# Reordering the scan of a Mamba-2 layer against its own state sums, its norm and its output projection

## The chip, the core and the metric

The kernel runs on one core of one Trainium2 chip. The metric is the device time of one execution in microseconds (us); three runs of the kernel before gave 1718.06, 1718.95 and 1721.03, median 1718.95. Times of single instructions come from one profiled execution.

## What is computed

One step of a two-layer backbone over 384 tokens (128 context tokens, then 256 latent tokens), width 1024. Layer 0 is FFN, latent attention, FFN; layer 1 is FFN, a bidirectional Mamba-2 scan (SSD), FFN. The change lies wholly in the scan. Cut to what matters:

```python
z, xbc, dt_raw = split(h @ w_in)              # h: normed input, 384 tokens
xbc = silu(conv5(xbc) + bias)                 # depthwise, then split into xs, B, C
dt  = softplus(dt_raw + dt_bias);  cum = cumsum(dt * a)      # per direction, per chunk of 128
y_diag = ((C B^T) * exp(seg(cum))) @ (xs * dt)               # inside a chunk, both directions
states = B^T @ (decay_end * dt * xs)                         # what a chunk adds to the state
h_next = h_in * exp(cum[-1]) + states                        # from chunk to chunk
y = y_diag + (C * exp(cum)) @ h_in + dsum * xs               # 2048 channels
out = rmsnorm(y * silu(z), norm_g) @ w_out                   # norm over the 2048 channels
```

The context is one chunk per direction, starting from zero; the latent tokens are two chunks, starting from a state that is given. The states of the context are an output.

## The kernel before, in words

Activations lie transposed: 128 channels on the partitions, 384 tokens along the free axis. Every weight passes through TensorE exactly once, from one stream of 512 KB units: SyncE loads a unit into `raw` (4 buffers), ScalarE rounds it into `whi` (L109), VectorE subtracts for the rest `wlo` (L110), 3 buffers each. `wmm` (L119 to L128) takes the 128 x 128 pieces of the stream in the order in which the program calls it and makes three products from each (L124, L125, L126); the host packs the weights in that order. An `in_tile` (L275) is 24 such products, one 128-channel tile of the input projection.

The 2048 channels of the scan are 16 tiles, `tau` = 0 to 15, of two heads each; four tiles share a group with one B and one C. The loop at L827 has steps `s` and is a software pipeline written out by hand:

- step `s` projects and convolves the x tile `s` (`conv`, L648, with L657 on VectorE; from step 2 on the projection of tile `s+1` is made ahead) and, every fourth step, the next group's B and C (`group_tiles`);
- `silu_z` evacuates and activates a z tile (L643, L791; table loads with it);
- `xtok(s-1)` transposes x to token order (L776), copies it (L778) and makes `xw`, weighted by decay, on GpSimd (L782);
- `mwork(s-1)` makes the decay matrix of a tile: three `seg` products (L765, L766), Exp on ScalarE (L767), two multiplications on VectorE (L768, L769), and C times decay into `cp` (L771);
- `ssd(s-2)` does all that is left of a tile: the state sums `pst` on TensorE (L801), their copy out, the next chunk's state `h1` on VectorE (L807, L809), and then at once the y products: those inside a chunk (L813), those with the given state `h` and those with `h1` (both L819). VectorE adds the skip term (L822), GpSimd multiplies with silu(z) into `yz` (L823);
- `loads(s)` asks SyncE for the next tile's decay rows (`segl`, `segr`), `cp` and `h0`.

In step 1 `dt_post` turns `dtt` (softplus, times a) into sums and decays: transposes (L714), small sums (L719, L720, L737 to L739), eight writes to `seg_d` (L730). After it come `loads(0, 1)`.

After the loop (L860 to L896): 16 pairs `yh`, `yl` of operands for the output projection (L864 on ScalarE, L865 on VectorE), then 16 squares (ScalarE, L869 and L872) that GpSimd adds into `yacc` (L873), then the projection `so`: the first 14 of 16 pieces of four output tiles, `rstd` after the third of them (its six small products are L216), `spread`, then the last two pieces of each and four whole tiles.

The program order is only a priority: a scheduler at compile time writes each engine's queue, taking what it reckons ready first. On the chip each engine then works its queue strictly in order.

Of the kernel before, what the change touches and what calls it, by code (L numbers as in the profile page):

```python
# [15 lines left out]
P = 128  # L16
# [37 lines left out]
def kernel(ctx, tc, xT_d, wstream, mod01, modw, crow_d, cst_d, tab_d, rope_d, ckvT_d, krT_d, h0_d,  # L54
# [11 lines left out]
    def bank(name):  # L66
        return psum.tile([P, 512], F32, tag="ps", name=name)
# [528 lines left out]
    def ssm(nxt):  # L596
# [11 lines left out]
        def mt(shape, tag, bufs=1, dt=F32):  # L608
            return sp.tile(shape, dt, tag=tag, name=tag, bufs=bufs)

        def keyf(m, k):
            return ("si", m, k)

        MZ, MX, MB, MC, MDT = 0, 16, 32, 36, 40
        dtt = mt([P, NTOK], "dtt")
        eb = mt([P, 3, 4, P], "E", 2)
        e1, e2, e3 = eb[:, 0].rearrange("p a b -> p (a b)")[:, 0:NTOK], eb[:, 1].rearrange("p a b -> p (a b)")[:, 0:NTOK], \
            eb[:, 2].rearrange("p a b -> p (a b)")[:, 0:NTOK]
        segr = [mt([P, 4, NTOK], f"segr{i}", 1, F32R) for i in range(2)]
        segl = [mt([P, NTOK], f"segl{i}", 1, F32R) for i in range(2)]  # L620
        ident16, mask16 = mt([P, P], "ident16", 1, BF16), mt([P, 4, P], "mask16", 1, BF16)

        def seg_init():
# [53 lines left out]
        tt(out=e2, in0=e2, in1=e1, op=ALU.mult)  # L677
        stt(out=dtt, in0=dtt, scalar=0.0, op0=ALU.max, in1=e2, op1=ALU.add)
        tt(out=dtt, in0=dtt, in1=e3, op=ALU.add)
        seg = mt([P, NTOK], "seg")  # L680
        ts(out=seg[64:128, :], in0=dtt[64:128, :], scalar1=1e-37, scalar2=None, op0=ALU.max)
        act(seg[64:128, :], seg[64:128, :], AF.Ln)
        seg_init()
# [21 lines left out]
            nc.scalar.copy(cb.rearrange("p a b -> p (a b)"), pc[:, 0:NTOK])  # L705
            grp[g] = [bT, cT, btok, cb]

        dtok = mt([P, 3, P], "dtok")
        dcy = mt([P, 2, 3, 32], "dcy")

        def dt_post():
            pt = bank("dtT")
            for c in range(3):
                nc.tensor.transpose(pt[:, c * P:(c + 1) * P], dtt[:, c * P:(c + 1) * P], T("ident"))  # L714
            nc.vector.tensor_copy(dtok.rearrange("p a b -> p (a b)"), pt[:, 0:NTOK])
            pr = bank("cumr")
            for c in range(3):
                da = dtok[:, c, 64:128]
                mm(pr[0:32, c * P:(c + 1) * P], da[:, 0:32], T("triu"), start=True, stop=True)  # L719
                mm(pr[32:64, c * P:(c + 1) * P], da[:, 32:64], T("tril"), start=True, stop=True)  # L720
            ecumr = mt([64, NLAT], "ecumr")
            segh, segt = mt([P, NTOK], "y", 2, F32R), mt([P, NTOK], "y", 2, F32R)
            nc.vector.tensor_copy(seg[0:64, :], pr[0:64, 0:NTOK])
            nc.scalar.copy(segh, seg)
            tt(out=segt, in0=seg, in1=segh, op=ALU.subtract)
            for half in range(2):
                for hl, s in ((0, segh), (1, segt)):
                    for d in range(2):
                        p0 = half * 64 + d * 32
                        nc.sync.dma_start(seg_d[:, half, hl, d], s[p0:p0 + 32, :].bitcast(F32))  # L730
            act(ecumr, pr[0:64, NCTX:NTOK], AF.Exp)
            nc.scalar.dma_start(ecum_d, ecumr)
            pc = bank("cum")
            for d, rest in enumerate(("slo", "sup")):
                cols = slice(64 + 32 * d, 96 + 32 * d)
                o = 96 * d
                mm(pc[:, o:o + 32], T(rest), dtok[:, 0, cols], start=True, stop=True)  # L737
                mm(pc[:, o + 32:o + 64], T(rest), dtok[:, 1 + d, cols], start=True, stop=True)
                mm(pc[:, o + 64:o + 96], T("ones"), dtok[:, 1 + d, cols], start=True, stop=True)  # L739
            act(dcy.rearrange("p a b c -> p (a b c)"), pc[:, 0:192], AF.Exp)  # L740
            for d in range(2):
                for ci, c in enumerate((0, 1 + d)):
                    tt(out=dcy[:, d, ci, :], in0=dcy[:, d, ci, :], in1=dtok[:, c, 32 * d:32 * d + 32], op=ALU.mult)
# [3 lines left out]
        def loads(*taus):  # L747
            for tau in taus:
                nc.sync.dma_start(segl[tau % 2][2:18, :].bitcast(F32), seg_d[tau].rearrange("a b c d t -> (a b c d) t"))
                nc.sync.dma_start(segr[tau % 2][0:2].bitcast(F32), seg_d[tau, 0].rearrange("b c d t -> b (c d) t"))  # L750
            for tau in taus:
                cp[tau] = mt([P, 2, 2, NLAT], "cp", 2)
                for d in range(2):
                    src = ecum_d[d * 32 + 2 * tau:d * 32 + 2 * tau + 2, :]
                    nc.sync.dma_start(cp[tau][:, d], src.partition_broadcast(P))
                h0[tau] = mt([P, 2, P], "h0", 2)
                nc.sync.dma_start(h0[tau], h0_d[:, :, tau * P:(tau + 1) * P])

        def mwork(tau):
# [27 lines left out]
        def silu_z(pz):  # L787
            tz = evac(pz)
            zs = mt([P, NTOK], "zs", 3)
            for s, a, b in SEGS:  # L790
                act(zs[:, a:b], tz[:, a:b], AF.Silu, bias=tz[:, NTOK + s:NTOK + s + 1])  # L791
            return zs

        def ssd(tau, zs):
            g = tau // 4
            btok = grp[g][2]
            w, xt, h = xw[tau], xtk[tau], h0[tau]
            pst = bank("st")
            for d in range(2):
                for ci, c in enumerate((0, 1 + d)):  # L800
# [2 lines left out]
            sto = mt([P, 2, P], "sto", 2)  # L803
            nc.scalar.copy(sto.rearrange("p a b -> p (a b)"), pst[:, 0:256])
            nc.sync.dma_start(state_d[:, :, tau * P:(tau + 1) * P], sto)
            h1 = mt([P, 2, P], "h1", 2)
            tt(out=h1.rearrange("p d (h q) -> p d h q", h=2), in0=h.rearrange("p d (h q) -> p d h q", h=2),  # L807
               in1=dcy[:, :, 2, 2 * tau:2 * tau + 2].unsqueeze(3).to_broadcast([P, 2, 2, 64]), op=ALU.mult)
            tt(out=h1.rearrange("p a b -> p (a b)"), in0=h1.rearrange("p a b -> p (a b)"), in1=pst[:, 256:512], op=ALU.add)  # L809
            py = bank("y")  # L810
            for c in range(3):
                for hh in range(2):
# [8 lines left out]
            y = mt([P, NTOK], "y", 2)  # L821
            stt(out=y, in0=xc[tau], scalar=dsum[:, tau:tau + 1], op0=ALU.mult, in1=py[:, 0:NTOK], op1=ALU.add)  # L822
            nc.gpsimd.tensor_tensor(out=yz[:, tau, :], in0=y, in1=zs, op=ALU.mult)  # L823

        group_tiles(0, pb, pc0)
        px = {0: px0}
        for s in range(NTAU + 2):  # L827
            if s < NTAU:
                if s % 4 == 0 and s > 0:
                    group_tiles(s // 4)  # L830
                xc[s] = mt([P, NTOK], "xc", 4)
                conv(px.pop(s) if s in px else in_tile(keyf, MX + s), s, xc[s])
                if s == 1:
                    z_first = [silu_z(in_tile(keyf, MZ))]
                    with tc.high_priority(60):
                        dt_post()
                    loads(0, 1)
                    z_first.append(silu_z(in_tile(keyf, MZ + 1)))
            if 2 <= s < NTAU - 1:
                px[s + 1] = in_tile(keyf, MX + s + 1)  # L840
            if s >= 2:
                zs = z_first[s - 2] if s < 5 else silu_z(in_tile(keyf, MZ + s - 2))
            if 1 <= s <= NTAU:
                if (s - 1) % 4 == 0:
                    group_post((s - 1) // 4)
                xtok(s - 1)
            if s == 2:
                z_first.append(silu_z(in_tile(keyf, MZ + 2)))
                mwork(0)
            if 2 <= s <= NTAU:  # L850
                mwork(s - 1)
            if s >= 2:
                ssd(s - 2, zs)
            if 2 <= s < NTAU:
                loads(s)
        inner.close()
        next_prep(nxt)
        gate = sec(layer, 5)
        yp = outer.enter_context(tc.tile_pool(name="ssmy", bufs=1, reuse_waits="tile"))
        yh, yl = [], []  # L860
        for k in range(NTAU):
            yh.append(yp.tile([P, NTOK], F32R, tag=f"yh{k}", name=f"yh{k}"))
            yl.append(yp.tile([P, NTOK], F32R, tag=f"yl{k}", name=f"yl{k}"))
            act(yh[k], yz[:, k, :], AF.Copy, scale=C("ssm_g", k))  # L864
            stt(out=yl[k], in0=yz[:, k, :], scalar=C("ssm_g", k), op0=ALU.mult, in1=yh[k], op1=ALU.subtract)  # L865

        for k in range(NTAU):
            if k == 0:
                act(yacc, yz[:, k, :], AF.Square)  # L869
            else:  # L870
                sq = yp.tile([P, NTOK], F32, tag="sqy", name="sqy", bufs=2)
                act(sq, yz[:, k, :], AF.Square)  # L872
                nc.gpsimd.tensor_tensor(out=yacc, in0=yacc, in1=sq, op=ALU.add)  # L873

        def so(ps, m, ks):
            for k in ks:
                wmm(ps[:, :NTOK], ("so", m, k), yh[k], yl[k], k == 0, k == NTAU - 1)

        def fin(m, ps):
            t = yp.tile([P, NTOK], F32, tag="t", name="tso", bufs=2)  # L880
            tt(out=t, in0=ps[:, :NTOK], in1=rext[:, :NTOK], op=ALU.mult)
            residual(m, t, gate, nxt)

        pso = [bank(f"so{m}") for m in range(4)]
        for m in range(4):
            so(pso[m], m, range(14))
            if m == 2:
                spread = rstd(yacc, 1.0 / 2048.0, rext[:, 0:NTOK])
        spread()
        for m in range(4):  # L890
# [211 lines left out]
```

## Time and profile before

| what | value |
|---|---|
| median of three runs | 1718.95 us |
| the profiled execution's own time | 1718.74 us |
| its span, first to last instruction | 1717.0 us |
| TensorE busy | 1662.9 us (97%) |
| VectorE busy | 1253.8 us (73%) |
| ScalarE busy | 798.2 us (46%) |
| GpSimd busy | 198.5 us (12%) |
| mean granted TensorE clock | 0.986 of full speed |

The 1.7 us between the profiled execution's time and its span lie outside the instructions. Busy time counts an engine as busy while an instruction of it runs; TensorE's own speed depends on the granted clock besides, which is shown for stretches of the span. The scan layer lies between about 1060 and 1400 us of the span.

### The profile page before, as it was taken

The page shows a single profiled execution, that of the slowest core. Times are in us where ns is not written, and L with a number is a line of the kernel's source. Part 1 is how long each engine was busy: PE and PEld are TensorE (multiplying, and loading weights), DVE is VectorE, ACT ScalarE, POOL GpSimd, SP SyncE. Part 2 cuts the span into 40 slices and gives each one's busy share as a digit, 9 for nine tenths or more (in the row PEclk, how much of TensorE's full clock was granted, in tenths as well). Part 3 has the DMA queues.
Part 4 walks back from the last instruction along what each step waited for, and adds up shares of the span by engine and source line. Part 5 has one row for each costly group of instructions (what it writes and reads, how often), then busy time and mean ns, then how long its engine had stood idle before and what let it go on. Part 6 is the DMA issues. An engine that isn't in the chain of part 4 may idle for free.

```text
span 1717.0 us, 25236 instructions
## 1 busy us (share of the span) xinstructions
PE 1662.9 (97%) x9616; PEld 1589.8 (93%) x9631; DVE 1253.8 (73%) x2069; ACT 798.2 (46%) x1312; POOL 198.5 (12%) x180
## 2 busy tenths in 40 slices
PE   7999999999999999999999999989999799999996
PEld 4899999978899999999999999878898799999996
DVE  3798889569768887976888896777877665444443
ACT  3534333455554333334333334877667744333332
POOL 0111100100001111000111000012212601111000
PEclk9999999999999999999999999899999999999998
DMA  8576666433246665765666674434444233333431
GB/s 345 172 230 211 209 206 219 132 137 111 76 170 188 203 207 190 231 211 173 204 208 203 200 229 150 123 105 132 128 139 120 84 124 122 123 125 124 132 124 49
DMA packets 88441, 281.99 MB, mean 164 GB/s; under 512 B 9836, under 2 KB 19900, under 8 KB 87808
## 3 DMA queue, kind: packets, MB, share of 16 engines
q1 hardware_dynamic: 86560, 274.26, 49.6%
q0 software_dynamic: 1104, 5.28, 0.9%
q8 instruction: 75, 1.23, 0.3%
q10 hardware_dynamic: 656, 0.85, 0.1%
q14 instruction: 46, 0.38, 0.1%
HBM read 276.06 MB, written 4.28 MB: 163 GB/s over the span
## 4 chain that ended last, share of the span: by engine, by line
PE 86%; DVE 5%; ACT 4%; DMA 2%; issue 2%; POOL 1%; SPq 0%; DVEq 0%; ACTq 0%; POOLq 0%
PE in L124 17%; PE in L126 17%; PE in L125 17%; PE fo L126 7%; PE fo L125 7%; PE fo L124 7%; DVE ca L657 2%; DMA cp<-ecum_d 1%; POOL yacc L873 1%; PE so L124 1%; PE so L125 1%; PE so L126 1%; ACT L767 1%; DVE wlo L110 1%; PE psmod L141 1%
## 5 line engine op out<-in xcount | busy, mean ns | idle before, releaser
L124 PE MATMUL in<-xh,wlo 128*128 128x386 f32 x1792 | 613.0, 343 | 3.1 <-ACT xh L246 3.1
L109 ACT CAST whi<-raw 128x1024 fp32r<-128x1024 f32 x348 | 365.2, 1050 | 539.2 <-issue 210.2
L126 PE MATMUL in<-xh,whi 128*128 128x386 f32 x1792 | 610.8, 341 | 0.0
L125 PE MATMUL in<-xl,whi 128*128 128x386 f32 x1792 | 607.9, 339 | 0.2 <-DVE xl L248 0.2
L110 DVE TENSOR_TENSOR wlo<-raw,whi 128x1024 fp32r<-128x1024 f32 x348 | 436.8, 1255 | 137.8 <-ACT whi L109 137.5
L124 PEld LDWEIGHTS in<-xh,wlo 128*128 128x128 f32 x1792 | 339.3, 189 | 10.9 <-issue 5.9
L125 PEld LDWEIGHTS in<-xl,whi 128*128 128x128 f32 x1792 | 340.0, 190 | 4.3 <-issue 1.8
L126 PEld LDWEIGHTS in<-xh,whi 128*128 128x128 f32 x1792 | 337.9, 189 | 4.9 <-issue 4.9
L125 PE MATMUL fo<-al,whi 128*128 128x384 f32 x704 | 236.7, 336 | 0.0
L124 PE MATMUL fo<-ah,wlo 128*128 128x384 f32 x704 | 236.7, 336 | 0.0
L126 PE MATMUL fo<-ah,whi 128*128 128x384 f32 x704 | 236.7, 336 | 0.0
L183 DVE CUSTOM_DVE_ANT_0 work<-modraw,crow,cst 128x1024 f32<-128x1024 f32 x144 | 185.2, 1287 | 21.7 <-POOL al L327 20.5
L327 POOL TENSOR_TENSOR al<-work,ah 128x384 fp32r<-128x384 f32 x88 | 109.5, 1244 | 739.4 <-ACT ah L326 726.0
L125 PEld LDWEIGHTS fo<-al,whi 128*128 128x128 f32 x704 | 132.0, 187 | 0.0
L126 PEld LDWEIGHTS fo<-ah,whi 128*128 128x128 f32 x704 | 132.0, 187 | 0.0
L124 PEld LDWEIGHTS fo<-ah,wlo 128*128 128x128 f32 x704 | 132.0, 187 | 0.0
L183 DVE CUSTOM_DVE_ANT_0 workout<-modraw,crow,cst 128x1024 f32<-128x1024 f32 x96 | 123.0, 1281 | 7.2 <-DMA modraw<-in_modw_dram 5.7
L326 ACT CAST ah<-work 128x384 fp32r<-128x384 f32 x88 | 45.3, 514 | 139.7 <-DVE work L324 139.7
L319 DVE TENSOR_TENSOR work<-in,rext 128x386 f32<-128x386 f32 x88 | 49.1, 558 | 67.6 <-PE in L126 65.8
L320 DVE TENSOR_TENSOR work<-in,rext 128x386 f32<-128x386 f32 x88 | 48.8, 554 | 45.3 <-PE in L126 45.3
L322 ACT ACTIVATE work<-work 128x128 f32<-128x128 f32 (+1 forms) x176 | 70.6, 447 | 6.0 <-DVE work L319 5.6
L324 DVE SCALAR_TENSOR_TENSOR work<-work 128x128 f32<-128x128 f32 (+1 forms) x176 | 68.0, 426 | 5.6 <-DVE work L320 0.5
(249 smaller groups left out, 1695.7 us busy)
## 6 DMA issues: line engine op xcount, KB each, us to landing
raw<-in_w_dram SPq DMA_DIRECT2D x348, 512.0 KB, 3.9
modraw<-in_modw_dram SPq DMA_DIRECT2D x128, 512.0 KB, 4.5
mod<-in_mod_dram SPq DMA_DIRECT2D x16, 512.0 KB, 9.5
cp<-ecum_d SPq DMA_DIRECT2D x32, 256.0 KB, 4.2
crow<-silu_d POOLq DMA_DIRECT2D x4, 1024.0 KB, 6.1
h<-in_h_dram SPq DMA_DIRECT2D x16, 128.0 KB, 4.3
out_dram<-sto SPq DMA_DIRECT2D x16, 128.0 KB, 2.2
xT<-in_xT_dram SPq DMA_DIRECT2D x4, 384.0 KB
```

What stands on the lines that cost most here:

```text
L109: nc.scalar.copy(his[u], raws[u])
L110: tt(out=los[u], in0=raws[u], in1=his[u], op=ALU.subtract)
L124: mm(out, wl, rh, start=start, stop=False)
L125: mm(out, wh, rl, start=False, stop=False)
L126: mm(out, wh, rh, start=False, stop=stop)
L183: nc.vector.tensor_tensor_reduce(out=junk(), in0=raw[n], in1=crow[:, s, :], scale=1.0, scalar=C("modb", j), op0=ALU.mult, op1=ALU.add, acc ...
L319: tt(out=g, in0=pg[:, :NX], in1=rext, op=ALU.mult)
L320: tt(out=u, in0=pu[:, :NX], in1=rext, op=ALU.mult)
L322: act(sg[:, a:b], g[:, a:b], AF.Silu, bias=g[:, NTOK + s:NTOK + s + 1])
L324: stt(out=sg[:, a:b], in0=u[:, a:b], scalar=u[:, NTOK + s:NTOK + s + 1], op0=ALU.add, in1=sg[:, a:b], op1=ALU.mult)
L326: nc.scalar.copy(ah[:, j, :], sg)
L327: nc.gpsimd.tensor_tensor(out=al[:, j, :], in0=sg, in1=ah[:, j, :], op=ALU.subtract)
```

## The change

The state sums and `h1` of a tile move out of `ssd` into `states(tau)`, which stays at the end of step `tau+2`; the rest, `scan_out(tau)`, moves to step `tau+3`, behind the x tile's projection, so that it comes half a step after the state sums. The z tiles move by a step or so (none in steps 4 and 9). In step 1 `dt_post` stands behind both z tiles instead of between them. The square of `yz` and its addition into `yacc` go into `scan_out`, so into the loop. `cp` and `h0` get a third buffer, paid for by laying `dtt`, `seg`, `ecumr` and `dtok` into buffers of `cp`. After the loop the operands of the first five pieces of the output projection go into the buffers of `segr` and `segl`, which are free by then; four output tiles take those five pieces, two tiles before the last y and two behind it. The rest of the projection follows as before, with `rstd` after the second tile instead of the third.

```diff
-        dtt = mt([P, NTOK], "dtt")
+        scr_a, scr_b = mt([P, 1024], "cp", 3), mt([P, 1024], "cp", 3)
+        dtt, seg, ecumr = scr_a[:, 0:NTOK], scr_a[:, NTOK:2 * NTOK], scr_a[0:64, 2 * NTOK:2 * NTOK + NLAT]
+        dtok = scr_b[:, 0:NTOK].rearrange("p (c t) -> p c t", c=3)
...
-                cp[tau] = mt([P, 2, 2, NLAT], "cp", 2)
+                cp[tau] = mt([P, 1024], "cp", 3).rearrange("p (d h t) -> p d h t", d=2, h=2)
...
-                h0[tau] = mt([P, 2, P], "h0", 2)
+                h0[tau] = mt([P, 2, P], "h0", 3)
...
-        def ssd(tau, zs):
-            g = tau // 4
-            btok = grp[g][2]
-            w, xt, h = xw[tau], xtk[tau], h0[tau]
+        def states(tau):
+            btok, w, h = grp[tau // 4][2], xw[tau], h0[tau]
             pst = bank("st")
...
             tt(out=h1.rearrange("p a b -> p (a b)"), in0=h1.rearrange("p a b -> p (a b)"), in1=pst[:, 256:512], op=ALU.add)
+
+        def scan_out(tau):
+            xt, h, h1, zs = xtk[tau], h0[tau], h1s.pop(tau), zst.pop(tau)
             py = bank("y")
...
             nc.gpsimd.tensor_tensor(out=yz[:, tau, :], in0=y, in1=zs, op=ALU.mult)
+            if tau == 0:
+                act(yacc, yz[:, tau, :], AF.Square)
+            else:
+                act(y, yz[:, tau, :], AF.Square)
+                nc.gpsimd.tensor_tensor(out=yacc, in0=yacc, in1=y, op=ALU.add)
...
+        def early_operands():
+            for i in range(2):
+                b = segbuf(i, 4, "segr", "yhl")
+                for j in range(2):
+                    yh[2 * i + j], yl[2 * i + j] = b[:, 2 * j], b[:, 2 * j + 1]
+            yh[EARLY - 1], yl[EARLY - 1] = (segbuf(i, 1, "segl", "yhl5")[:, 0] for i in range(2))
+            for k in range(EARLY):
+                out_operand(k)
...
-        for s in range(NTAU + 2):
+        for s in range(NTAU + 1):
...
                 if s == 1:
-                    z_first = [silu_z(in_tile(keyf, MZ))]
+                    z_tile(0)
+                    z_tile(1)
                     with tc.high_priority(60):
                         dt_post()
                     loads(0, 1)
-                    z_first.append(silu_z(in_tile(keyf, MZ + 1)))
             if 2 <= s < NTAU - 1:
                 px[s + 1] = in_tile(keyf, MX + s + 1)
-            if s >= 2:
-                zs = z_first[s - 2] if s < 5 else silu_z(in_tile(keyf, MZ + s - 2))
-            if 1 <= s <= NTAU:
+            if s == 3:
+                pz = in_tile(keyf, MZ + 3)
+            if s >= 3:
+                scan_out(s - 3)
+            if s == 3:
+                zst[3] = silu_z(pz)
+            if s >= 5 and s != 9:
+                z_tile(s - 1 if s < 9 else s - 2)
+            if s >= 1:
                 if (s - 1) % 4 == 0:
                     group_post((s - 1) // 4)
                 xtok(s - 1)
...
-            if 2 <= s <= NTAU:
+            if s >= 2:
                 mwork(s - 1)
-            if s >= 2:
-                ssd(s - 2, zs)
+                states(s - 2)
             if 2 <= s < NTAU:
                 loads(s)
+        early_operands()
+        z_tile(NTAU - 1)
+        scan_out(NTAU - 2)
+        states(NTAU - 1)
+        for m in range(2):
+            pso.append(bank(f"so{m}"))
+            so(pso[m], m, range(EARLY))
+        scan_out(NTAU - 1)
+        for m in range(2, 4):
+            pso.append(bank(f"so{m}"))
+            so(pso[m], m, range(EARLY))
         inner.close()
...
         for m in range(4):
-            so(pso[m], m, range(14))
-            if m == 2:
+            so(pso[m], m, range(EARLY, 14))
+            if m == 1:
                 spread = rstd(yacc, 1.0 / 2048.0, rext[:, 0:NTOK])
```

## Rows read from the trace of the kernel before

**Rows 1.** Stretches: start:end, length, busy time by engine (instructions), TensorE clock, DMA share, GB/s

```profile
1060.00:1400.00 340.00, 313.10 (x2018) 286.46 (x2032) 250.23 (x384) 237.58 (x398) 71.88 (x63) 0.96 0.40 120
1130.00:1344.00 214.00, 203.29 (x1410) 182.23 (x1422) 162.78 (x220) 154.56 (x262) 46.91 (x42) 1.00 0.43 127
1090.00:1100.00 10.00, 10.00 (x49) 9.62 (x46) 4.74 (x9) 9.35 (x16) 0.00 (x0) 0.65 0.49 143
1370.00:1380.00 10.00, 7.22 (x33) 7.23 (x34) 4.38 (x11) 4.99 (x7) 2.56 (x3) 0.66 0.31 105
```

**Rows 2.** Waits of TensorE, 1050 to 1400 us: total us, times, longest

```profile
PE y L819 <- DVE h L809: 10.2, 11, 1.8
PE y L813 <- DVE E L769: 6.8, 2, 6.5
PE rs L216 <- POOL yacc L873: 5.2, 1, 5.2
PE dtT L714 <- DVE dtt L684: 3.0, 1, 3.0
PE cumr L719 <- DVE dtok L715: 0.7, 1, 0.7
PE so L125 <- DVE yl L865: 0.6, 2, 0.3
PE so L124 <- ACT yh L864: 0.4, 1, 0.4
```

**Rows 3.** Timeline around step 1: start us, duration us, engine, line, operation, tiles [idle before]

```profile
1095.25 0.40 ACT L659 ACTIVATE xc<-ca 128x256 f32<-128x256 f32 x1
1099.98 0.14 PEld L776 LDWEIGHTS xt<-tab,xc 128*128 128x128 f32 x1
```

**Rows 4.** Timeline, first y: a projection tile, state sums, y products

```profile
1109.46 0.34 PE L125 MATMUL in<-xl,whi 128*128 128x386 f32 x1
1113.36 0.34 PE L126 MATMUL in<-xh,whi 128*128 128x386 f32 x1
1116.30 1.05 PE L801 MATMUL st<-xw,btok 128*128 128x128 f32 x8
1123.83 1.55 PE L813 MATMUL y<-E,xtk 128*64 128x128 f32 x12 [6.48 <-DVE E L769]
1125.14 1.95 PE L819 MATMUL y<-cp,h 128*64 128x128 f32 x16
```

**Rows 5.** Timeline, two steps of the loop and the tail: state sums, h1, y products

```profile
1216.63 1.05 PE L801 MATMUL st<-xw,btok 128*128 128x128 f32 x8
1227.77 0.41 DVE L809 TENSOR_TENSOR h<-h,st 128x256 f32<-128x256 f32 x1
1232.89 1.05 PE L801 MATMUL st<-xw,btok 128*128 128x128 f32 x8
1233.88 0.88 PE L813 MATMUL y<-E,xtk 128*64 128x128 f32 x12
1238.49 0.41 DVE L809 TENSOR_TENSOR h<-h,st 128x256 f32<-128x256 f32 x1
1339.77 0.66 PE L819 MATMUL y<-cp,h 128*64 128x128 f32 x8 [1.65 <-DVE h L809]
1343.09 0.66 PE L819 MATMUL y<-cp,h 128*64 128x128 f32 x8 [0.79 <-DVE h L809]
```

**Rows 6.** The chain of waits (GpSimd) and VectorE's timeline, norm additions: start us, duration us

```profile
1358.01 1.03 POOL yacc L873
1359.11 1.89 POOL yacc L873
1353.66 1.21 DVE L110 TENSOR_TENSOR wlo<-raw,whi 128x1024 fp32r<-128x1024 f32 x1
1358.37 1.75 DVE L110 TENSOR_TENSOR wlo<-raw,whi 128x1024 fp32r<-128x1024 f32 x1 [3.50 <-ACT whi L109]
```

**Rows 7.** Timeline of ScalarE: the one square inside the loop

```profile
1129.58 0.53 ACT L869 ACTIVATE yacc<-yz 128x384 f32<-128x384 f32 x1 [4.71 <-POOL yz L823]
```

More of the change, by code (lines that the diff above doesn't have):

```diff
@@ L618, in ssm, with segbuf @@
             eb[:, 2].rearrange("p a b -> p (a b)")[:, 0:NTOK]
-        segr = [mt([P, 4, NTOK], f"segr{i}", 1, F32R) for i in range(2)]
-        segl = [mt([P, NTOK], f"segl{i}", 1, F32R) for i in range(2)]
+        def segbuf(i, n, tag, name):
+            return op_.tile([P, n, NTOK], F32R, tag=f"{tag}{i}", name=f"{name}{i}")
+        segr = [segbuf(i, 4, "segr", "segr") for i in range(2)]
+        segl = [segbuf(i, 1, "segl", "segl")[:, 0] for i in range(2)]
         ident16, mask16 = mt([P, P], "ident16", 1, BF16), mt([P, 4, P], "mask16", 1, BF16)
@@ L679, in ssm @@
         tt(out=dtt, in0=dtt, in1=e3, op=ALU.add)
-        seg = mt([P, NTOK], "seg")
         ts(out=seg[64:128, :], in0=dtt[64:128, :], scalar1=1e-37, scalar2=None, op0=ALU.max)
@@ L706, in group_post @@
             grp[g] = [bT, cT, btok, cb]
-        dtok = mt([P, 3, P], "dtok")
         dcy = mt([P, 2, 3, 32], "dcy")
@@ L720, in dt_post @@
                 mm(pr[32:64, c * P:(c + 1) * P], da[:, 32:64], T("tril"), start=True, stop=True)
-            ecumr = mt([64, NLAT], "ecumr")
             segh, segt = mt([P, NTOK], "y", 2, F32R), mt([P, NTOK], "y", 2, F32R)
@@ L792, in silu_z @@
             return zs
-        def ssd(tau, zs):
-            g = tau // 4
-            btok = grp[g][2]
-            w, xt, h = xw[tau], xtk[tau], h0[tau]
+        h1s = {}
+        def states(tau):
+            btok, w, h = grp[tau // 4][2], xw[tau], h0[tau]
             pst = bank("st")
@@ L805, in ssd @@
             nc.sync.dma_start(state_d[:, :, tau * P:(tau + 1) * P], sto)
-            h1 = mt([P, 2, P], "h1", 2)
+            h1 = h1s[tau] = mt([P, 2, P], "h1", 2)
             tt(out=h1.rearrange("p d (h q) -> p d h q", h=2), in0=h.rearrange("p d (h q) -> p d h q", h=2),
@@ L823, in ssd, with out_operand, so, z_tile @@
             nc.gpsimd.tensor_tensor(out=yz[:, tau, :], in0=y, in1=zs, op=ALU.mult)
+            if tau == 0:
[3 more added lines that the diff above has]
+                nc.gpsimd.tensor_tensor(out=yacc, in0=yacc, in1=y, op=ALU.add)
+        yh, yl, pso = {}, {}, []
+        def out_operand(k):
+            act(yh[k], yz[:, k, :], AF.Copy, scale=C("ssm_g", k))
+            stt(out=yl[k], in0=yz[:, k, :], scalar=C("ssm_g", k), op0=ALU.mult, in1=yh[k], op1=ALU.subtract)
+        def early_operands():
[6 more added lines that the diff above has]
+                out_operand(k)
+        def so(ps, m, ks):
+            for k in ks:
+                wmm(ps[:, :NTOK], ("so", m, k), yh[k], yl[k], k == 0, k == NTAU - 1)
+        def z_tile(tau):
+            zst[tau] = silu_z(in_tile(keyf, MZ + tau))
+        EARLY = 5
+        zst = {}
         group_tiles(0, pb, pc0)
         px = {0: px0}
-        for s in range(NTAU + 2):
+        for s in range(NTAU + 1):
             if s < NTAU:
@@ L847, in ssm @@
             if s == 2:
-                z_first.append(silu_z(in_tile(keyf, MZ + 2)))
+                z_tile(2)
                 mwork(0)
-            if 2 <= s <= NTAU:
+            if s >= 2:
                 mwork(s - 1)
-            if s >= 2:
-                ssd(s - 2, zs)
+                states(s - 2)
             if 2 <= s < NTAU:
                 loads(s)
+        early_operands()
[9 more added lines that the diff above has]
+            so(pso[m], m, range(EARLY))
         inner.close()
@@ L859, in ssm @@
         yp = outer.enter_context(tc.tile_pool(name="ssmy", bufs=1, reuse_waits="tile"))
[L860 to L877, printed above, removed]
+        for k in range(EARLY, NTAU):
+            yh[k] = yp.tile([P, NTOK], F32R, tag=f"yh{k}", name=f"yh{k}")
+            yl[k] = yp.tile([P, NTOK], F32R, tag=f"yl{k}", name=f"yl{k}")
+            out_operand(k)
         def fin(m, ps):
@@ L882, in fin @@
             residual(m, t, gate, nxt)
-        pso = [bank(f"so{m}") for m in range(4)]
         for m in range(4):
-            so(pso[m], m, range(14))
-            if m == 2:
+            so(pso[m], m, range(EARLY, 14))
+            if m == 1:
                 spread = rstd(yacc, 1.0 / 2048.0, rext[:, 0:NTOK])
```

## The prediction

> **What bounds the kernel now.** I looked first at the busy shares: TensorE works 97% of the span, and every weight passes through it once in either kernel. The change neither adds nor removes a product, so all that can be won is time in which TensorE stands or runs at its lower clock, and that has to be sought in the scan layer. The stretches come next [rows 1]: from 1060 to 1400 us TensorE is busy 313.1 of 340.0 us, so it stands for 26.9 us. The waits of TensorE [rows 2] account for all of it: 10.2 + 6.8 + 5.2 + 3.0 + 0.7 + 0.6 + 0.4 = 26.9. This makes the sum simple: each row of that list is a term, and I ask of each whether the new order covers it. The clock comes on top: behind the first and the last of the long waits the stretches show a mean of 0.65 and 0.66 of full speed over 10 us, against 1.00 over the whole loop [rows 1]. As the clock has two levels, 1.2 and 2.4 GHz, that is 7.0 and 6.8 of 10 us at the lower one.
>
> So a change that left TensorE no wait here would win 26.9 us and what the clock took, and no more.
>
> **Part 1, step 1 (`dt_post` behind both z tiles).** TensorE stands 3.0 us for `dtt` and 0.7 for `dtok` [rows 2]. From 1090 to 1100 it is busy all the time with 7.0 us at half clock, which loses 3.5 us; with the small sums just before, 4.0 (an estimate). A projection tile is 24 products at 0.177 us apart, 4.2 us (23 of them span 1109.46 to 1113.36) [rows 4]. With one more in front, the 3.0 us are covered. What is late next is `xtok(0)`. The work in front of it is the same as before, so without these losses TensorE would reach it 3.7 + 4.0 = 7.7 us before 1099.98, at 1092.3. But the `xc` of tile 0 leaves ScalarE only at 1095.25 + 0.40 = 1095.65 [rows 3], and ScalarE is busy 9.35 of those 10 us [rows 1]. So 3.4 us come back as a new wait, unless ScalarE's queue changes. Net **4.3 us**; bounds 0 (the new wait costs the clock too) and 7.7.
>
> **Part 2, the first y half a step later.** The longest single wait, 6.5 of the 6.8 us, is that of the first y product for `E` of tile 0 [rows 2, 4]. Behind it the products run slow: twelve in 1.55 us that take 0.88 in the loop, and sixteen in 1.95 where eight take 0.66 [rows 4, 5], which is 1.3 us, and 1.6 with the next few. In the new order two projection tiles (x 4 and z 3) stand between the state sums of tile 0 and its y. The data came 1123.83 - 1116.30 = 7.5 us after the sums began [rows 4]; the cover is 1.0 + 8.4 = 9.4 us. Net **8.1 us**; bounds 6.5 (the clock falls elsewhere) and 8.1.
>
> **Part 3, `h1` in the loop.** Of the 10.2 us, two waits of 1.65 and 0.79 stand at the tail [rows 5] and are counted in part 4; 7.8 us are here. Why is `h1` late? L809 itself takes 0.41 us, but it stands in VectorE's queue behind L768, which waits for the next tile's Exp on ScalarE. From the start of the state sums to the end of L809 it takes 6.0 us in a plain step (1232.89 to 1238.90) and 11.6 in a step with B and C (1216.63 to 1228.18) [rows 5]; TensorE's queue already has projection products in between. In the new order the cover is at least the sums (1.0), an x tile (4.2) and the y products that need no `h1` (0.9 and some 0.5): 6.6 us. That holds for the plain step, not for the long ones, unless the z tile stands in front too (10.8 us, still 0.8 short of 11.6). I take **4 us** won, about half. Bounds: 7.8 (all covered), and a loss of 12: eight of the thirteen steps take longer than the cover, the longest by 5.0 us, so at half of that on average 8 x 2.5 = 20 us in place of 7.8.
>
> The third buffers of `cp` and `h0` let SyncE ask for the next tile about half a step sooner. No wait of TensorE names `cp`, so nothing is booked. SyncE issues the same loads and none is moved past the weight stream. Laying `dtt` and the others into buffers of `cp` makes `cp` of tile 1 wait for the write of `ecumr`, which its source needs anyway: nothing.
>
> **Part 4, the tail and the output projection.** The norm's 5.2 us [rows 2] go: behind the last y only the last multiplication, square and addition are left, under 4 us, while early products of two output tiles (30 products, 5.2 us) and then two tiles' next nine pieces run ahead of `rstd`. With them goes the low clock: 6.8 us of 1370 to 1380, of which TensorE stood 2.8, so 4.0 us at half speed, 2.0 lost [rows 1]. The last `h1` waits (1.65 + 0.79 = 2.4 us), the operand waits (0.6 + 0.4) and the short wait for E (0.3) have a z tile and 60 early products as cover. The ten early operands can be written once the last `seg` products have read `segr`, while that z tile runs. What is late next is the operand of piece 5, whose space the scan's own tiles must leave first; I book 1.0 us. Net 5.2 + 2.0 + 2.4 + 1.0 + 0.3 - 1.0 = **9.9 us**; bounds 7 and 10.9.
>
> **Part 5, what comes into the loop.** Per tile a square (0.5 us) on ScalarE [rows 7] and an addition (1.0 us) on GpSimd [rows 6]. ScalarE is busy 154.6 of 214.0 us there, VectorE 162.8, GpSimd 46.9 [rows 1]; as busy time they fit. As waits they may not. The square waits for GpSimd, and behind it in ScalarE's queue stand the rounding of weights, Silu and Exp. The one square that already runs in the loop made ScalarE stand 4.7 us [rows 7]. And GpSimd's additions disturb VectorE: where one meets `wlo`, the addition took 1.89 us instead of 1.03, and `wlo` 1.75 instead of 1.21 [rows 6], so VectorE loses 0.5 us each time. It looks as if one waits for the other: the addition of 1358.01 ends at 1359.04, `wlo` goes on from 1358.37 to 1360.12, and the addition behind it takes 0.86 us more. Fifteen times 0.5 are 8 of VectorE's 51 us of idle. I book **2 us** lost on TensorE for both; bounds 0 and 15.
>
> The Trainium skill, "SBUF — State Buffer", in its definition of the shared port pair, says that VectorE and GpSimd hold that pair as an exclusive lock for a whole instruction, and that the loser fully blocks. The trace of that collision agrees in kind, with 0.5 and 0.9 us of delay. By that rule an addition can block VectorE for its whole 1.0 us; fifteen of them are 15 us in place of 2, and the time would be 1707.
>
> **The sum.** 4.3 + 8.1 + 4 + 9.9 - 2 = 24.3 us. The profiled execution took 1718.74 us (span 1717.0 and 1.7 around it), 0.2 us under the median of 1718.95, so the two can stand for each other: **1694.4 us**.
>
> **Rivals.**
> (a) *The wait for `h1` grows.* The y products come at 6.6 us behind the sums where `h1` takes up to 11.6. For it: the long step of rows 5. Against it: today's queue has a second tile in between there. Part 3 is then -12 instead of +4: 1710.
> (b) *GpSimd's additions stand on the chain.* Each of the fifteen delays VectorE's `h1` or E by its full 1.0 us, 15 us instead of 2: 1707. For it: rows 6. Against it: VectorE idles a quarter of the loop.
> (c) *The square stops ScalarE, and the kernel gets slower.* ScalarE works 154.6 / 15 = 10.3 us of a step of 214 / 15 = 14.3; with the square 10.8. Where it also stands behind GpSimd, the step grows by what goes over 14.3. Parts 1, 2 and 4 (22.3 us) are eaten up, over 15 steps, when a step takes 15.8 us, so the point is 5.0 us of standing per step. At the 4.7 seen, a step takes 15.5: +18 - 22.3, so 1714; at 6.0, 16.8: +37 - 22.3, so 1733. For it: rows 7. Against it: the square of rows 7 stood at the loop's start, ahead of its time in the queue, and a later one can have work in front of it.
> (d) *The queues stay as they are.* The scheduler, which takes what it reckons ready, puts the y products where they were, so that parts 1 to 3 bring nothing: 1718.7 - 9.9 + 2 = 1711.
>
> **How the numbers follow.** Forecast 0.64, (a) 0.13, (b) 0.08, (c) 0.09, (d) 0.06. All upper bounds together give 7.7 + 8.1 + 7.8 + 10.9 = 34.5 us, so 1684; the range begins a little above. It goes up to 1711, over (a), (b) and (d), and leaves out (c) and the worst ends of the others. Measurements of this kernel tell 0.2%, 3.4 us, from no change. Faster by more: the forecast, (b), and most of (a) and (d), 0.87; slower: (c) past its point and the worst of (a), 0.07; between, 0.06.
>
> **What would show it.** In the waits of TensorE, `rs` for `yacc` and the 6.5 us for `E` should be gone, `h1` should be under 4 us, and a wait of 2 to 4 us for `xc` should stand where `xtok(0)` is. The clock should be 1.00 in the tail. If ScalarE's waits for `yz` sum to over 40 us, (c) is at work; if the waits for `h1` grow, (a), or (b) where VectorE's instructions in front of L809 are longer as well. A time above 1711 would show the forecast wrong, by a wait in a place that I have not named.

## The result, and the profile after

| | before | after |
|---|---|---|
| median | 1718.95 us (3 runs) | 1696.24 us (4 runs, 1695.77 to 1696.92) |
| the profiled execution, its span | 1718.74, 1717.0 us | 1695.77, 1694.0 us |
| TensorE busy | 1662.9 us | 1655.4 us |
| mean granted clock | 0.986 | 0.991 |

A fourth execution of the kernel before took 5813.8 us and is left out of its median. The ratio of the times is 0.9861, with a 95% interval of 0.985 to 0.9873: 1.4% faster, 23 us of span, of which 21.7 lie in the scan layer, from the norm products in front of it (L216, 1061.0 before, 1059.6 after) to the ones that spread its own norm (L229, 1382.8 and 1359.7). 1694.4 us had been forecast.

The waits of TensorE in the changed kernel, 1050 to 1400 us (total us, times, longest), answer to [rows 2]; L824 was L819, L811 was L809, L818 was L813, L717 was L714:

```profile
PE y L824 <- DVE h L811: 9.0, 7, 3.8
PE dtT L717 <- DVE cp L688: 1.5, 1, 1.5
PE y L818 <- DVE E L771: 0.7, 1, 0.7
PE in L124 <- DVE t L648: 0.5, 1, 0.5
```

26.9 us have become 11.7. `rs` and the operands of the output projection are gone from the list, `E` has lost its 6.5 us. The waits for `h1` in the loop have not become less: of the 10.2 us, 7.8 lay there and 2.4 at the tail, and now it is 9.0. The stretches of the changed kernel (columns as in [rows 1]) show the same:

```profile
1060.00:1400.00 340.00, 328.14 (x2142) 303.82 (x2158) 262.88 (x398) 239.48 (x407) 67.79 (x63) 0.98 0.42 129
1090.00:1100.00 10.00, 10.00 (x66) 9.97 (x67) 7.83 (x18) 9.45 (x16) 0.00 (x0) 1.00 0.52 152
1270.00:1280.00 10.00, 6.22 (x35) 5.40 (x32) 4.88 (x7) 7.19 (x12) 0.73 (x1) 0.74 0.30 99
1280.00:1290.00 10.00, 9.46 (x54) 8.55 (x54) 5.52 (x7) 7.98 (x14) 3.33 (x4) 0.92 0.39 138
```

Behind step 1 the clock is 1.00 where it was 0.65. In the loop, where it had been 1.00, there is now a dip to 0.74 at 1270, and a shorter one around 1310 (0.94 and 0.88 in the stretches 1300 and 1310). ScalarE's and GpSimd's waits of the changed kernel, 1130 to 1340 us, show what is new there (L832 is the square, L833 the addition):

```profile
ACT y L832 <- POOL yz L828: 27.6, 13, 4.7
POOL yacc L833 <- ACT y L832: 12.7, 14, 3.0
```

How the dip at 1270 comes about stands in its timeline (start us, duration us, engine, line):

```profile
1260.67 1.93 POOL L828 TENSOR_TENSOR yz<-y,zs 128x384 f32<-128x384 f32 x1 [13.28 <-DVE y L827]
1261.65 1.38 DVE L662 SCALAR_TENSOR_TENSOR ca<-u,cst,ca 128x386 f32<-128x386 f32 x1
1263.24 1.01 POOL L833 TENSOR_TENSOR yacc<-yacc,y 128x384 f32<-128x384 f32 x1 [0.64 <-ACT y L832]
1263.28 2.31 DVE L662 SCALAR_TENSOR_TENSOR ca<-u,cst,ca 128x386 f32<-128x386 f32 x2
1267.71 0.31 ACT L663 ACTIVATE xc<-ca 128x128 f32<-128x128 f32 x1 [3.23 <-DVE ca L662]
1269.64 0.60 ACT L769 ACTIVATE E<-seg 128x512 f32<-128x512 f32 x1
1270.25 1.28 ACT L793 ACT_TABLE_LOAD   x1
1271.55 0.80 ACT L793 ACTIVATE zs<-t 128x128 f32<-128x128 f32 x2
1272.37 1.28 ACT L769 ACT_TABLE_LOAD   x1
1273.66 1.08 ACT L769 ACTIVATE E<-seg 128x512 f32<-128x512 f32 x2
1274.78 0.96 DVE L770 TENSOR_TENSOR E<-E 128x768 f32<-128x768 f32 x1 [5.03 <-ACT E L769]
1275.65 0.41 DVE L811 TENSOR_TENSOR h<-h,st 128x256 f32<-128x256 f32 x1
1276.12 1.12 PE L824 MATMUL y<-cp,h 128*64 128x128 f32 x8 [3.78 <-DVE h L811]
```

The convolution products of VectorE (L662, 0.61 us each where GpSimd is idle) take 1.38 and twice 1.15 us beside GpSimd's work. ScalarE stands 3.2 us for the convolution, with the Exp of another tile queued behind. That Exp comes in three pieces, and ScalarE's queue has the Silu of a z tile (L793) between the first and the other two: each of these two changes comes with a table load of 1.28 us, so that 3.4 us lie between the pieces. VectorE stands 5.0 us for the last piece with L811 queued behind it, and TensorE 3.8 us for L811.

### The profile page after: what moved, and what is told of

It reads as the page before. It is cut to its first block, busy times and chain, and to the rows that moved or that the text cites. A ratio compares the mean times of both kernels' runs of the same rounds, so it can differ in the third digit from the quotient of the medians.

```text
span 1694.0 us, 25203 instructions
## 1 busy us (share of the span) xinstructions
PE 1655.4 (98%) x9616; PEld 1584.6 (94%) x9631; DVE 1254.1 (74%) x2069; ACT 791.7 (47%) x1308; POOL 196.1 (12%) x180
## 4 chain that ended last, share of the span: by engine, by line
PE 88%; DVE 5%; ACT 4%; DMA 2%; issue 1%; SPq 0%; POOL 0%; DVEq 0%; ACTq 0%
PE in L124 17%; PE in L126 17%; PE in L125 17%; PE fo L124 7%; PE fo L126 7%; PE fo L125 7%; DVE ca L662 2%; DMA cp<-ecum_d 2%; PE so L124 1%; PE so L125 1%; PE so L126 1%; ACT L769 1%; PE psmod L141 1%; PE wo L124 1%; PE pv L548 1%
## 5 line engine op out<-in xcount | busy, mean ns | idle before, releaser
L109 ACT CAST whi<-raw 128x1024 fp32r<-128x1024 f32 x348 | 365.3, 1050 | 526.2 <-issue 227.0
L110 DVE TENSOR_TENSOR wlo<-raw,whi 128x1024 fp32r<-128x1024 f32 x348 | 430.5, 1237 | 129.9 <-ACT whi L109 129.6
L327 POOL TENSOR_TENSOR al<-work,ah 128x384 fp32r<-128x384 f32 x88 | 111.2, 1263 | 749.6 <-ACT ah L326 736.2
```

The costliest lines, as they stand in the source:

```text
L109: nc.scalar.copy(his[u], raws[u])
L110: tt(out=los[u], in0=raws[u], in1=his[u], op=ALU.subtract)
L327: nc.gpsimd.tensor_tensor(out=al[:, j, :], in0=sg, in1=ah[:, j, :], op=ALU.subtract)
```

## The experiments

Twelve kernels ran, each in three rounds beside the kernel before. Every edit gives all queues a new order at compile time, so a run shows its edit together with what the scheduler made of it. All times are medians; "slower" and "faster" are against the 1696.2 us of the changed kernel, and behind each time stands its ratio to the kernel before with the 95% interval. Each interval is some 2.5 us to either side, so a difference of less than about 3 us between two of these kernels is not shown.

**e1: the norm sum behind the loop again.**

```diff
-                act(y, yz[:, tau, :], AF.Square)
-                nc.gpsimd.tensor_tensor(out=yacc, in0=yacc, in1=y, op=ALU.add)
...
+        for k in range(NTAU):      # behind all operands, as before the change
```

> The changed kernel with the squares and their additions put back behind the loop. By the prediction's terms the wait of the rs products for yacc and the low clock behind it return (5.2 + 2.0 us) and the loop is freed of 2: about 1701 us, up to 1706 if the wait is longer because rstd now comes one output tile earlier. Rival (the squares and additions cost the loop as much as the norm's wait was worth): 1696 or less.

1697.8 us, 0.9872 (0.9855 to 0.9888): 1.6 slower, which the intervals do not tell from no difference. Its waits of TensorE:

```profile
PE rs L216 <- POOL yacc L916: 9.6, 1, 9.6
PE y L824 <- DVE h L811: 3.4, 5, 1.3
PE dtT L717 <- DVE cp L688: 1.5, 1, 1.5
PE y L818 <- DVE E L771: 0.7, 1, 0.7
```

The wait of `rs` is back, with 9.6 us, and 5.6 us of the `h1` waits are gone. Moving the norm into the loop has therefore brought no gain that can be told from the noise: it paid with `h1` for what it won at `rs`. The time is nearer to the rival's (1696 or less) than to the 1701 us expected.

**e2: no norm sum at all** (the squares and additions of tiles 1 to 15 are deleted).

> The changed kernel without 15 of the 16 squares and without the additions: that part of the norm is left out, so that only the price of them in the loop goes. Prediction (2 us on TensorE): 1694 us. Rival (the 30.5 us for which ScalarE stands behind GpSimd's yz, and the delays of VectorE, reach h1 and from there TensorE): 1684 to 1690, with the waits for h1 under 3 us and the clock at 1.00 all through the loop. If nothing: 1696.

1685.1 us, 0.9794 (0.9779 to 0.9808): 11.1 faster. The waits for `h1` are 3.5 us, and the clock is 1.00 in every stretch of 10 us in the scan. Time and clock are the rival's; its waits for `h1` were to be under 3 us. 6.0 of the 11.1 us are waits, and TensorE's busy time is 5.2 less (1655.4 to 1650.2).

**e9 and e10: the squares alone, the additions alone.**

```diff
-                act(y, yz[:, tau, :], AF.Square)
-                nc.gpsimd.tensor_tensor(out=yacc, in0=yacc, in1=y, op=ALU.add)
+                act(y, yz[:, tau, :], AF.Square)                                                   # e9
+                nc.gpsimd.tensor_tensor(out=yacc, in0=yacc, in1=yz[:, tau, :], op=ALU.add)         # e10
```

> The changed kernel with the squares in the loop but without GpSimd's additions: the sum of squares is left out. With e2 (neither: 1685.1) and the changed kernel (both: 1696.2) it parts the price. If ScalarE's standing for yz is the cost: 1693 to 1696, with some 30 us of that standing and h1 waits of 8 or more. If GpSimd's additions are the cost, by what they do to VectorE: 1685 to 1688, although ScalarE stands as long.

> The changed kernel with GpSimd's additions in the loop but without the squares (yz itself is added, so the sum of squares is left out). If the additions' delays of VectorE are the cost: 1693 to 1696, with VectorE's conv products (L662) near 770 ns instead of 697. If ScalarE's standing is the cost: 1685 to 1688.

1690.4 us (0.9832, 0.9817 to 0.9846) and 1689.0 us (0.9822, 0.9807 to 0.9836). Both times lie between the two ranges expected. Against the 1685.1 of neither, the squares cost 5.3 us and the additions 3.9, and both together 11.1: neither alone is the cause. The waits of ScalarE in e9, then VectorE's groups between 1125 and 1320 us in e2 and in e10 (busy us, mean ns | idle before):

```profile
ACT y L832 <- POOL yz L828: 27.2, 13, 4.7
```

```profile
L662 DVE SCALAR_TENSOR_TENSOR ca<-u,cst,ca 128x386 f32<-128x386 f32 x74 | 50.8, 697 | 2.6 <-ACT ca L660 2.2
L110 DVE TENSOR_TENSOR wlo<-raw,whi 128x1024 fp32r<-128x1024 f32 x29 | 36.1, 1245 | 0.5 <-ACT whi L109 0.5
```

```profile
L662 DVE SCALAR_TENSOR_TENSOR ca<-u,cst,ca 128x386 f32<-128x386 f32 x75 | 53.9, 728 | 2.6 <-ACT ca L660 2.2
L110 DVE TENSOR_TENSOR wlo<-raw,whi 128x1024 fp32r<-128x1024 f32 x29 | 39.3, 1356 | 0.5 <-ACT whi L109 0.5
```

The additions lengthen VectorE's instructions: in e9, without them, the two groups stay at 700 and 1263 ns, and in the changed kernel, with both, L662 is at 767 ns. The squares act through ScalarE's queue, but it is not shown that the standing for `yz` is what counts there. In front of the dip, at about 1260 us, ScalarE stands only 1.3 us for it, in the changed kernel as in e9. What differs from the kernels without squares is the order of the queue, here in e2:

```profile
1262.25 0.60 ACT L769 ACTIVATE E<-seg 128x512 f32<-128x512 f32 x1
1262.87 1.28 ACT L663 ACT_TABLE_LOAD   x1
1264.64 0.31 ACT L663 ACTIVATE xc<-ca 128x128 f32<-128x128 f32 x1 [0.49 <-DVE ca L662]
1265.97 1.28 ACT L769 ACT_TABLE_LOAD   x1
1267.26 1.09 ACT L769 ACTIVATE E<-seg 128x512 f32<-128x512 f32 x2
1269.73 0.66 PE L824 MATMUL y<-cp,h 128*64 128x128 f32 x8 [0.19 <-DVE h L811]
```

In e2 the first piece of Exp stands in front of the convolution's `xc` (L663) instead of behind it, and the last piece ends 3.1 us after `xc` instead of 6.4. So it is in e1, e2, e10, e11 and e12, where TensorE waits 0.2 to 0.9 us for `h1` at this place; in the changed kernel, e4, e5, e8 and e9 it stands behind, and the wait is 2.7 to 3.8 us. That is 3.6 of the 5.5 us by which the changed kernel waits longer for `h1` than e2. e11 even has a square just there (L903 at 1257.92 us), but one whose `yz` is long ready. No run has a square that stands for `yz` and the order of e2, so the two are not parted.

**e3: the y of a tile directly behind its state sums.**

```diff
-            if s >= 3:
-                scan_out(s - 3)
...
                 states(s - 2)
+                scan_out(s - 2)
```

> The changed kernel with the y of a tile directly behind its state sums again, at the end of the same step; all else kept. Prediction's terms: 8.1 us of the first y and 4 of h1 come back, so 1708 us, with a wait of some 6 us for E of tile 0 and h1 waits of about 10. Rival (the scheduler fills these places with projection products anyway, and the gain was that of the tail, of step 1 and of the norm): 1697 to 1700.

1702.8 us, 0.9898 (0.9884 to 0.9913): 6.6 slower, where 1708 had been expected.

```profile
PE y L818 <- DVE E L771: 9.3, 1, 9.3
PE y L824 <- DVE h L811: 7.9, 7, 1.8
```

The first y waits 9.3 us, but `h1` no more than in the changed kernel. With the norm in the loop, the half step is worth the first y, and less than that wait, since other places lost a little of theirs.

**e4: no early operands and products.** All 16 operands stand behind the loop.

> The changed kernel without the early operands and early products: all 16 operands behind the loop. Prediction's terms: the last h1 and operand waits return, 2.4 + 1.0 + 0.3 us, so 1700. Rival (the y of the last tile has nothing at all in front of it now: its E, h1, skip term, silu product and operand come one after the other): 1704 to 1708 with a wait of over 5 us at the start of the output projection.

1703.8 us, 0.9906 (0.9891 to 0.9921): 7.5 slower, just under the rival's range, and its long wait is 4.4 us where over 5 had been named.

```profile
PE so L124 <- ACT yh L838: 4.4, 1, 4.4
```

```profile
1330.00:1340.00 10.00, 5.89 (x20) 5.82 (x21) 7.40 (x13) 7.37 (x16) 2.98 (x3) 0.58 0.14 50
1340.00:1350.00 10.00, 10.00 (x54) 10.00 (x54) 6.84 (x16) 5.25 (x8) 0.00 (x0) 0.91 0.16 54
```

That is one wait of 4.4 us; and of the 8.4 + 1.8 us at half clock TensorE was busy for 6.1, which loses 3 more.

**e5: `dt_post` between the z tiles.**

```diff
                     z_tile(0)
-                    z_tile(1)
                     with tc.high_priority(60):
                         dt_post()
                     loads(0, 1)
+                    z_tile(1)
```

> The changed kernel with dt_post between the z tiles again. Prediction's terms: 3.7 us of waits and about 4.0 of low clock return, less the wait for xc that I had feared (3.4, not seen in the changed kernel's trace): 1700.5 to 1704 us. Rival (the order on the queues has moved for other reasons, buffers above all, and the wait is gone without the move): 1696.

1706.4 us, 0.9928 (0.9913 to 0.9942): 10.2 slower, past the expectation.

```profile
PE y L824 <- DVE h L811: 12.8, 7, 4.9
PE dtT L717 <- DVE cp L688: 3.0, 1, 3.0
PE cumr L722 <- ACT cp L686: 0.8, 1, 0.8
```

The old waits of 3.0 and 0.8 us return, and the clock from 1090 to 1100 is 0.67 again; that makes about 6 us. The rest is `h1`, which stands 3.8 us longer in the new order of the queues. The two can't be kept apart in this run.

**e6: the state sums ahead of the next tile's matrix.**

```diff
-                mwork(s - 1)
                 states(s - 2)
+                mwork(s - 1)
```

> The changed kernel with states(s-2) ahead of mwork(s-1), so that h1 (L811) is no longer behind L770, which waits for Exp, in VectorE's queue. If the place in the queue is why h1 is late, the 9.0 us of waits for h1 and most of the low clock after them (some 5 us) go: 1684 to 1688 us. Rival (something behind h1 is late instead, the state sums for xw, or E): 1693 to 1697, with a new wait for E or xw.

1696.9 us, 0.9874 (0.986 to 0.9889): no gain. `h1` waits 6.2 instead of 9.0 us, but projection products now wait 3.6 us for VectorE (`in` for L827), and ScalarE stands 34.9 us for `yz` (30.5 in the changed kernel). The time is the rival's, with another wait than it named. So the place of L811 behind L770 is not by itself what costs the time; that the whole chain is late fits, but is not shown.

**e7: y without `h1`.**

```diff
-            for hs, last in ((h, False), (h1, True)):
+            for i, hs in enumerate((h, h)):
```

> The changed kernel whose y products take the given state h in place of h1: h1 is still computed, but y leaves its update out. It shows the most that h1's lateness costs. If h1 alone holds TensorE in the loop: 1683 to 1687 us and no wait over 1 us there. Rival (E, or the y products' own order, is as late as h1): 1692 or more, with waits for E in place of h1.

The y products take the given state `h` in place of `h1`. 1682.1 us, 0.979 (0.9775 to 0.9804): 14.1 faster, a little more than expected, with no wait over 0.8 us left in the loop. So nearly all that still held TensorE came to it through `h1`.

**e8: each square and addition one step later.**

> The changed kernel with each square and addition one step later, so that ScalarE finds yz ready. If ScalarE's standing behind GpSimd (30.5 us in sum) is what the norm costs in the loop: that falls under 8 us, and the time to 1688 to 1693. Rival (VectorE's delays by GpSimd's additions are the cost, and these stay): 1695 to 1697 in spite of it.

1691.0 us, 0.9838 (0.9822 to 0.9855): 5.3 faster, in the expected span, but by less than the expected way: ScalarE still stands 23.7 us for `yz` (30.5 in the changed kernel, both with the first tile's 2.9), not under 8. `h1` waits 6.9 us; 3.5 us of the gain are TensorE's busy time (1655.4 to 1651.9). One step of program order is less than a step in the queue.

**e11 and e12: the norm sum behind the loop, its additions on VectorE.** e11 puts it behind the last y in the program, so that the scheduler fills gaps with it (five of its fifteen squares come before 1300 us, the first at 1258); e12 behind all operands.

```diff
+        for k in range(NTAU):
+            if k == 0:
+                act(yacc, yz[:, k, :], AF.Square)
+            else:
+                sq = mt([P, NTOK], "bT", 2)
+                act(sq, yz[:, k, :], AF.Square)
+                tt(out=yacc, in0=yacc, in1=sq, op=ALU.add)
```

> The changed kernel with the squares behind the last y in the program, so in gaps of ScalarE near the end of the scan, and with the additions on VectorE instead of GpSimd. If both prices of the norm in the loop are avoided and the sum is still done when rstd asks for it: 1685 to 1688 us, below both kernels, with no wait of rs over 2 us. Rival (the sum comes too late, as with GpSimd behind the loop, or the additions hold up the last y): 1692 to 1698.

> As the run with the squares and additions behind all operands (1697.8, rs waited 9.6 us), but with the additions on VectorE: 0.55 us each instead of 1.0 and more. If the chain of additions is what rs waited for, the wait shrinks from 9.6 us to 2 to 5 and the time to 1688 to 1692. Rival (ScalarE's operands and squares are the chain, not the additions): over 7 us of wait, 1695 to 1698.

e11: **1685.3 us**, 0.9799 (0.9783 to 0.9816), as expected; e12: 1686.6 us, 0.9808 (0.9794 to 0.9823), better than expected. Both beat both kernels, with the full computation. TensorE's waits in e11, then the one for `rs` in e12:

```profile
PE y L824 <- DVE h L811: 3.4, 5, 1.5
PE dtT L717 <- DVE cp L688: 1.5, 1, 1.5
PE y L818 <- DVE E L771: 0.7, 1, 0.7
PE so L125 <- DVE yl L834: 0.5, 1, 0.5
```

```profile
PE rs L216 <- DVE yacc L916: 0.5, 1, 0.5
```

e12 against e1 shows that GpSimd's additions were what `rs` waited for: the same place, the other engine, 0.5 us instead of 9.6, and 11.2 us of time.

## Why the prediction was right

The time, 1696.2, lies 1.8 us from the forecast, and the frame held in the main: of the 21.7 us won in the scan, 15.2 are rows of TensorE's list of waits, and some 4 are products that no longer run at the lower clock (from busy time and granted clock in steps of 1 us, that clock cost 8.5 us before and 4.4 after, an estimate). But the closeness of the total is luck. With what the runs give for each part (6.2, 7.4, 4.3, 10.9 and -11.1), the gain would be 17.7 us; 22.7 were measured. The other 5 us belong to no part: 1.4 lie in front of the scan, some 2.5 are busy time of TensorE in the scan that the granted clock does not explain, and where they and the rest come from stays open. They made up for more than half of the 9 us by which part 5 was too small.

- **Part 1 (4.3 us).** The trace gives more: 3.7 us of waits became 1.5, and the 4.0 booked for the clock came back whole, 6.2 us. The wait for `xc` that I had taken off did not come. The row read for it [rows 3] was of ScalarE's old queue; in the new one `xc` of tile 0 stands ahead of the Exp of `ecumr` and its table load, and is done at 1092.1, not 1095.65; the changed kernel's timeline of ScalarE:

```profile
1091.66 0.40 ACT L664 ACTIVATE xc<-ca 128x256 f32<-128x256 f32 x1
1092.48 1.28 ACT L733 ACT_TABLE_LOAD   x1
```

- **Part 2 (8.1 us).** The 6.5 us became 0.7, and the products run at full clock, booked at 1.6: 7.4. e3 agrees, as its first y waits 9.3 us.
- **Part 4 (9.9 us).** All of its waits are gone and the clock is 1.00: 10.9 by the rows, as the 1.0 us booked against it did not come. But the rows say little of why. e1 shows that the norm's 5.2 us were not won by moving the sum into the loop, since that cost as much; e4 shows the early products to be worth 7.5 us, for which I had some 3.7.
- **Part 3 (4 us) and part 5 (-2).** Taken together I forecast +2; the trace shows the loop's `h1` waits going from 7.8 to 9.0 us, where the prediction's sign was under 4, and two new dips of the clock. e2 parts them: without the norm the `h1` waits are 3.5 us, so part 3 is 4.3, as booked; no run has the y joined without the norm, so the half step is not parted from the new z order and the third buffers. The price of the norm in the loop was 11.1 us and not 2. **This is the term that failed**, within its bounds of 0 and 15. I had set 8 us of VectorE's time against its 51 us of idle, and called 2 us likely because both engines had room as busy time. e9 and e10 show why that is no measure. VectorE's lengthening was sized about right (0.031 x 75 + 0.111 x 29 = 5.5 us in the two groups shown), but it ends, like what the squares do to ScalarE's queue, on the one chain, convolution, Exp, L770, L811, that TensorE waits for. The waits for `h1` add up: 3.3 us longer than in e2 for the squares, 1.9 for the additions, 5.5 for both.

In e10 one addition begins beside `cp`'s product on VectorE:

```profile
1263.52 2.08 POOL L832 TENSOR_TENSOR yacc<-yacc,yz 128x384 f32<-128x384 f32 x1
1263.50 1.22 DVE L773 TENSOR_TENSOR cp<-cp,cT 128x1024 f32<-128x1024 f32 x1 [0.94 <-DMA cp<-ecum_d]
1264.64 1.37 DVE L662 SCALAR_TENSOR_TENSOR ca<-u,cst,ca 128x386 f32<-128x386 f32 x1
```

GpSimd's 2.08 us are about VectorE's 1.1, up to its next instruction, and its own 1.0; that next instruction then takes 1.37 us instead of 0.61. The fifteen additions cost 3.9 us in all. By the rule that the prediction took from the Trainium skill, "SBUF — State Buffer", in its definition of the shared port pair, by which the loser fully blocks, they could have cost 15 us. The trace of this collision is near to that rule, and the time is not: that either engine may be the one to wait, and that VectorE had idle time, would account for it, but no run tests that.

Of the rivals, (b) was there in part. Of (c) the standing was there, 2.0 us per step (30.5 / 15), under the 5.0 from which (c) decides. (a) and (d) were not: the later y did not make `h1` worse by itself (e2), and the order did change.

## What to carry to other kernels

When a unit that has idle time is given more work, ask who stands in its queue behind the wait that comes with it, and what the new instruction does to the order of that queue; the room in its busy share says nothing of either. Where an in-order engine would have to wait for a slower one in every step, put the work where it is not waited for (here in gaps towards the end of the scan or behind it, with the additions on VectorE): the same sum cost 11 us in the loop with the additions on GpSimd, and there 0.2 and 1.6 us (e11 and e12 against e2), which is within the noise. And a move that takes out one wait may be paid for by another: try it alone, as e1 does, before it is called a gain.

## What was not expected of the hardware

- Waits of 2.7 (e9), 3.0, 3.8, 4.4, 5.2 and 6.5 us were each followed by a stretch at the lower clock, and so was one of 1.7 us in the changed kernel (0.50 from 1309 to 1312 us). One of 1.85 us in the kernel before and one of 3.1 us in e8 were not: the clock stayed at 1.00. So the length of a wait alone does not tell it, and what else does is not shown.
- With the 15.2 us of waits, 7.5 us of TensorE's busy time went, for the same products; some 4 of them are the lower clock.
- The squares and the additions cost 5.3 and 3.9 us alone and 11.1 together; the 1.9 us above the sum are within the noise. In the traces the lower clock took 4.4 us from TensorE with both, 1.7 with the squares alone and none with the additions alone (estimates as above).
